# Order of PSUM copies, weight splits and side work in the mixer of a one-core transformer layer

## The chip, the cores and the metric

One core of a Trainium2 chip runs the whole layer as one program. TensorE (PE), VectorE (DVE), ScalarE (ACT), GpSimd (POOL) and SyncE (SP) each work through an instruction queue of their own and meet at semaphores. The metric is device time in microseconds (us), lower is better; a measurement of the kernel is the median of several executions.

## The reference

A "macaron" layer for one sequence of 256 tokens and width 2048: a gated feed-forward block (ffn1), a token mixer and a second feed-forward block (ffn2), each fed through a layer norm that is shifted and scaled by vectors computed from a conditioning vector `c`.

```python
ada = (silu(c) @ w_ada + b_ada)[:, None, :]            # 2048 x 18432
sh1, sc1, g1, sh2, sc2, g2, sh3, sc3, g3 = split(ada, 9)
h = swiglu(modulate(x, sh1, sc1), ffn1_w_in, ffn1_w_out)       # inner width 5632
x = layernorm(ALPHA * x + 0.5 * (1 + g1) * h, ln1_g, ln1_b)
h = token_mixer(modulate(x, sh2, sc2), w_in, ..., w_out)
x = layernorm(ALPHA * x + (1 + g2) * h, ln2_g, ln2_b)
h = swiglu(modulate(x, sh3, sc3), ffn2_w_in, ffn2_w_out)
x = layernorm(ALPHA * x + 0.5 * (1 + g3) * h, ln3_g, ln3_b)

def token_mixer(h, ...):
    z = h @ w_in       # columns: fox q, k, v, f; mLSTM q, k, v, i, f, o
    y_fox = 8 heads of causal softmax attention (width 128) with a decay from cumsum(log_sigmoid(f))
    hm    = 4 heads of chunked mLSTM (width 256; causal conv and silu on q and k), rms-normed
    y     = concat(y_fox, sigmoid(o) * hm)
    return y @ w_out
```

Everything is in float32.

## The kernel before

**Products.** Every product is made from split operands: `split` writes a rounded part `hi` (ACT, L142) and the rest `lo = x - hi` (DVE, L143), and `mm3` adds three products hi·hi, hi·lo, lo·hi (L373 to L375). Weights stream from memory once, one megabyte per `load_w`: SP issues the transfer into one of three `raw` buffers, ACT and DVE split it into `hi` and `lo` tiles of a ring of six. `cols_form_a` uses weights as the stationary operand (256 columns per block of eight rows of 128), `cols_form_b` uses the activations as the stationary operand (blocks of four rows of 128; column groups of two halves [256, 264], so that the small gate columns ride along, or of one half [512]).

**PSUM.** Five banks (`pm`) hold the sums of the big products and three (`pa`, `aux_tile`) everything small. A column group of `cols_form_b` with two halves takes four of the five `pm` banks, so the next group finds one bank free and gets the others as the group before is copied out by `use_fv`, `use_mv` or, for the first group, by the eight sigmoids of L1144, which empty the banks of the mLSTM gate product `mo`.

**The ada vectors.** `w_ada` is contracted on DVE: an accumulation `acc += silu(c)[k] * w_ada[k]` (L157) for each 512 KB row piece, sixteen per part of 1024 columns, then a split and a sum over partitions by PE (`bc`, L170). ffn1's first vectors are made by `first_ada` during the first stage, where ffn1's first 3072 columns (12 groups of 512) are multiplied in four passes over a quarter of the depth each (`first_in`, passes j = 0 to 3; in passes 1 to 3 the add of L749 empties the banks). All others hang on a queue that `pump(rate)` moves on at each weight block; rates are R_F, R_IN and so on, a PAUSE ends a pump early and its debt is carried over. `need(n)` forces the queue on until n parts are done: `need(6)` before j = 9 of ffn2's first half. `pinned()` wraps queue work and adds order edges behind the last noted instructions in `pin`.

**The mixer's side work.** Generators in the list `side` (gates, convolution, mLSTM heads, rms norm, mLSTM outputs, fox heads) are advanced two steps per weight block by `step()`. A generator that yields True waits and does not count. A fox head has three steps: scores `lps` and softmax, transposes `ptp`, value product `yps`. `until(names)` advances in pairs until named steps are done; it is called for buffers and by `before(k)`, ahead of each block of the output projection, for rows k and k + 1 of its input. The projection's rows of the fox heads are split into `yhi` and `ylo`, whose pool takes the place of the mixer's input `xT`.

**Order.** A scheduler orders each engine's queue by estimated readiness and program order. `tc.issue_after(ins)` adds edges: what the block issues on the engine of `ins` comes behind it in that queue, without waiting for its end. `keep_in_program_order` puts an instruction behind everything traced before it on its engine.

Of the kernel before, what the change touches and what calls it, by code (L numbers as in the profile page):

```python
# [34 lines left out]
def layer_kernel(  # L35
# [324 lines left out]

    def load_w(src, nk, w, name):
        raw = wp.tile([P, nk, w], F32, tag="raw", bufs=3, name=f"raw_{name}")
        SP.dma_start(raw, src.rearrange("(k p) n -> p k n", p=P))
        h = nk // 2 if nk * w <= 2048 else nk // 4
        for q in range(nk // h):
            hi = wp.tile([P, h, w], F32R, tag="hi", bufs=6, name=f"hi_{name}{q}")
            lo = wp.tile([P, h, w], F32R, tag="lo", bufs=6, name=f"lo_{name}{q}")
            pin["w"] = split(raw[:, q * h:(q + 1) * h, :], hi, lo).ins
            for kk in range(h):
                yield q * h + kk, hi[:, kk, :], lo[:, kk, :]  # L370
# [6 lines left out]

    def cols_form_a(src, c0, outs, xT, name, npump, halves=(0, 1)):
        xhi, xlo = xT
        for kh in halves:  # L380
            for k8, hi, lo in load_w(src[kh * 1024:(kh + 1) * 1024, c0:c0 + 256], 8, 256, f"{name}_{kh}"):
                k = kh * 8 + k8
                for f in range(2):
                    fs = slice(f * P, (f + 1) * P)
                    mm3(outs[f], hi[:, fs], lo[:, fs], xhi[:, k, :], xlo[:, k, :],
                        k == 8 * halves[0], k == 8 * halves[-1] + 7)
            npump()

# [224 lines left out]

    def cols_1024(raws, xs, split_, load, ps, xT, npump, u0, u1):
        for a in range(2):
            for u, raw in enumerate(raws):
                for q in range(2):
                    k = 2 * u + q
                    for b in range(2):
                        PE.matmul(ps[a, b], xs[a, k], raw(q, b), start=k == 2 * u0, stop=False)  # L620
        for u in range(u0 + len(raws), u1):
            for k, hi, lo in split_.get(u) or load(u):
                for a in range(2):
                    ts_ = slice(a * P, (a + 1) * P)
# [15 lines left out]

    R_F, R_IN, R_OUT, R_MX, R_A, R_B = 1.25, 1.2, 1, 1.42, .9, .6
    NP = 2
# [90 lines left out]
    def first_in(j, i, ws):  # L733
# [9 lines left out]
        for b, ps in enumerate(pss):  # L743
            f0 = 2 * NS * gu + 4 * q + 2 * b
            part = first_part(f0, f0 + 2).rearrange("p f t -> p (f t)")
            if j == 0:
                S.copy(part, ps)
            else:
                V.tensor_tensor(out=part, in0=part, in1=ps, op=ALU.add)  # L749
# [95 lines left out]


    mps = {(a, b): mm_tile(f"mo{a}{b}") for a in range(2) for b in range(2)}
    with tc.issue_after(fence.ins):
        cols_1024(raws, xs, mow, mo_load, mps, xT, at(R_MX), 0, 8)
    npool.release()  # L850
# [15 lines left out]


    side = []
    done = set()

    def advance(n):
        for g in list(side):
            if n == 0:
                break
            got = next(g, 0)
            if got == 0:
                side.remove(g)
            n -= got is not True

# [4 lines left out]

    def step():
        pump(R_MX)
        advance(NP)

# [4 lines left out]

    def cols_form_b(c0, col, ws, use, name):
        ps = {(a, b): mm_tile(f"b_{name}{col}{a}{b}") for b in range(len(ws)) for a in range(2)}
        cb = [sum(ws[:b]) for b in range(len(ws) + 1)]
        for u in range(4):
            for k4, hi, lo in load_w(W[u * 512:(u + 1) * 512, c0 + col:c0 + col + cb[-1]], 4, cb[-1],
                                     f"{name}{col}_{u}"):
                k = u * 4 + k4  # L900
                for a in range(2):
                    ts_ = slice(a * P, (a + 1) * P)
                    for b in range(len(ws)):
                        bs = slice(cb[b], cb[b + 1])
# [24 lines left out]

    def form_a_pair(ca, cb, name):  # L930
        ps = [mm_tile(f"pr_{name}{i}") for i in range(2)]
        cols_form_a(W, ca, [p[:, :T] for p in ps], xT, f"{name}a", step)
        cols_form_a(W, cb, [p[:, T:] for p in ps], xT, f"{name}b", step)
        return ps
# [4 lines left out]
    def use_fv(col, a, ps, w):  # L939
        wv = min(w, 1024 - col)  # L940
        S.copy(yF[:, col // P:(col + wv) // P, a * P:(a + 1) * P], ps[:, :wv].rearrange("p (h n) -> p h n", n=P))
        if wv < w:
            S.copy(gz[:, a, 0:8], ps[:, wv:w])
# [11 lines left out]
    def fox_head(qs, h):  # L955
# [20 lines left out]
        done.add(f"qs{h}")  # L976
        yield
        tps = aux_tile(f"ptp{h}")
        for i in range(3):
# [20 lines left out]
    def use_mv(col, a, ps, w):  # L1000
        wv = min(w, 1024 - col)
        for i in range(0, wv, MV):
            S.copy(yM[(col + i) // MV][:, a, :MV], ps[:, i:i + MV])
# [138 lines left out]
    for a in range(2):  # L1142
        for h in range(NMH):
            S.activation(og[h][:, a, :MV], mps[a, h // 2][:, h % 2 * MV:(h % 2 + 1) * MV], AF.Sigmoid)  # L1144
    cols_form_b(C_FV, 512, [256, 264], use_fv, "fv")
# [24 lines left out]
    for j in (2, 3, 0, 1):  # L1170
        ps = form_a_pair(C_FQ + j * 256, C_FK + j * 256, f"f{j}")
        for i in range(2):
# [4 lines left out]
            side.append(fox_head(qs, h))  # L1177
    cols_form_b(C_FV, 0, [512], use_fv, "fv")
    done.add("fv0")
# [165 lines left out]
```

## Time and profile before

| | |
|---|---|
| three runs | 1955.89, 1961.45, 1962.55 us; median 1961.45 |
| profiled execution | 1965.73 us, its span 1964.0 us |
| granted TensorE clock, mean | 0.993 |
| busy us: PE, DVE, ACT, POOL | 1894.8, 1495.0, 962.6, 41.1 |
| read from memory | 506.71 MB, 259 GB/s over the span |
| mixer, us from the start | input products 843 to 1106, output projection 1110 to 1198 |

The page gives busy time per engine and the waits; a wait is idle time of an engine and the instruction that ended it. A busy PE need not be PE at its full rate: the start-to-start time of its products and the granted clock show that.

### The profile page before, as it was taken

Reading aid. Unit: us, or ns where it says so; the run is one execution under the profiler, and the core shown is the slowest. Engines: PE = TensorE matmul, PEld = TensorE weight load, DVE = VectorE, ACT = ScalarE, POOL = GpSimd, SP = SyncE. Lnnn points to the kernel's source line nnn. Section 1 sums busy time; section 2 is a strip of 40 time slices with the busy share of each in tenths; the row PEclk is TensorE's granted clock in tenths of the full one; section 3 lists DMA queues with packets and bytes.
Section 4 is the critical chain, followed back from the end, with each engine's and each line's share of the span. In section 5 each row is a group of like instructions: output and inputs, shape, how many; then the busy total and the mean of one; then the engine's idle time right before and its main releaser. Section 6 shows DMA issues by size and latency. Waiting matters only on the chain.

```text
span 1964.0 us, 32295 instructions
## 1 busy us (share of the span) xinstructions
PE 1894.8 (96%) x13057; PEld 1726.1 (88%) x13057; DVE 1495.0 (76%) x1878; ACT 962.6 (49%) x1396; POOL 41.1 (2%) x65
## 2 busy tenths in 40 slices
PE   3999999999999999999999998999999999999997
PEld 3999999999988887588999786899999999988885
DVE  7788988777788997677888688767766655555776
ACT  4554454444444554745655544555444444444553
POOL 1211100000000000000000000000000000000000
PEclk9999999999999999999999999999999999999998
DMA  9988878899999785489888784888777765655552
GB/s 351 356 302 293 318 243 290 287 312 315 298 323 322 266 301 173 149 303 299 269 300 278 268 282 157 291 280 278 241 248 250 259 217 190 235 193 193 193 193 86
DMA packets 295677, 510.90 MB, mean 260 GB/s; under 512 B 10818, under 2 KB 158690, under 8 KB 294504
## 3 DMA queue, kind: packets, MB, share of 16 engines
q1 hardware_dynamic: 287752, 480.53, 72.5%
q0 software_dynamic: 7776, 28.32, 4.0%
q8 instruction: 102, 1.67, 0.3%
q14 instruction: 47, 0.39, 0.1%
HBM read 506.71 MB, written 2.10 MB: 259 GB/s over the span
## 4 chain that ended last, share of the span: by engine, by line
PE 82%; DVE 7%; DMA 6%; issue 2%; ACT 2%; SPq 0%; DVEq 0%; POOL 0%; ACTq 0%; POOLq 0%
PE gu_f L373 8%; PE gu_f L375 8%; PE o_f L373 8%; PE gu_f L374 8%; PE o_f L375 8%; PE o_f L374 8%; DMA ar<-in_w_ada_dram 4%; PE s L373 3%; PE s L375 3%; PE s L374 3%; DVE acc L157 2%; PE fs L373 1%; PE fs L374 1%; PE fs L375 1%; PE o_mx L373 1%
## 5 line engine op out<-in xcount | busy, mean ns | idle before, releaser
L157 DVE SCALAR_TENSOR_TENSOR acc<-ar,csil,acc 128x1024 f32<-128x1024 f32 x242 | 307.6, 1272 | 83.2 <-DMA ar<-in_w_ada_dram 82.2
L373 PE MATMUL s<-xhi_f,hi_s 128*128 128x256 f32 x768 | 213.9, 280 | 3.0 <-DVE hT L749 1.3
L375 PE MATMUL s<-xhi_f,lo_s 128*128 128x256 f32 x768 | 213.2, 278 | 0.0
L374 PE MATMUL s<-xlo_f,hi_s 128*128 128x256 f32 x768 | 213.1, 278 | 0.0
L375 PE MATMUL gu_f<-xhi_f,lo_f2i 128*128 128x256 f32 x768 | 212.0, 276 | 0.0
L373 PE MATMUL gu_f<-xhi_f,hi_f2i 128*128 128x256 f32 x768 | 212.0, 276 | 0.0
L374 PE MATMUL gu_f<-xlo_f,hi_f2i 128*128 128x256 f32 x768 | 212.0, 276 | 0.0
L143 DVE TENSOR_TENSOR lo_f2i<-raw_f2i,hi_f2i 128x1024 fp32r<-128x1024 f32 x96 | 117.5, 1224 | 91.6 <-ACT hi_f2i L142 91.6
L373 PE MATMUL gu_f<-xhi_f,hi_f1i 128*128 128x256 f32 x640 | 176.8, 276 | 0.3 <-DVE hT L749 0.3
L375 PE MATMUL gu_f<-xhi_f,lo_f1i 128*128 128x256 f32 x640 | 176.7, 276 | 0.0
L374 PE MATMUL gu_f<-xlo_f,hi_f1i 128*128 128x256 f32 x640 | 176.7, 276 | 0.0
L142 ACT CAST hi_f2i<-raw_f2i 128x1024 fp32r<-128x1024 f32 x96 | 100.8, 1050 | 135.4 <-PE gu_f L374 124.6
L142 ACT CAST hi_s<-raw_s 128x1024 fp32r<-128x1024 f32 x96 | 99.7, 1051 | 113.5 <-PE s L374 60.4
L373 PEld LDWEIGHTS s<-xhi_f,hi_s 128*128 128x128 f32 x768 | 145.3, 190 | 3.7 <-DVE hT L749 1.5
L375 PEld LDWEIGHTS s<-xhi_f,lo_s 128*128 128x128 f32 x768 | 145.1, 189 | 0.3 <-DVE lo_s L143 0.3
L374 PEld LDWEIGHTS s<-xlo_f,hi_s 128*128 128x128 f32 x768 | 145.3, 189 | 0.0
L373 PEld LDWEIGHTS gu_f<-xhi_f,hi_f2i 128*128 128x128 f32 x768 | 144.2, 188 | 0.2
L374 PEld LDWEIGHTS gu_f<-xlo_f,hi_f2i 128*128 128x128 f32 x768 | 144.2, 188 | 0.2
L375 PEld LDWEIGHTS gu_f<-xhi_f,lo_f2i 128*128 128x128 f32 x768 | 144.2, 188 | 0.0
L142 ACT CAST hh<-hT 128x512 fp32r<-128x512 f32 x130 | 80.1, 623 | 130.2 <-PE o_f L374 128.8
L143 DVE TENSOR_TENSOR lo_f2o<-raw_f2o,hi_f2o 128x1024 fp32r<-128x1024 f32 x88 | 107.7, 1224 | 44.9 <-ACT hi_f2o L142 44.8
L373 PE MATMUL o_f<-hi_f2o,hh 128*128 128x512 f32 x344 | 135.2, 393 | 0.0
(453 smaller groups left out, 5400.6 us busy)
## 6 DMA issues: line engine op xcount, KB each, us to landing
ar<-in_w_ada_dram SPq DMA_DIRECT2D x240, 512.0 KB, 5.4
raw_s<-in_ffn_w_in_dram SPq DMA_DIRECT2D x48, 1024.0 KB, 7.5
raw_f2i<-in_ffn_w_in_dram SPq DMA_DIRECT2D x48, 1024.0 KB, 5.1
raw_f1o<-in_ffn_w_out_dram SPq DMA_DIRECT2D x44, 1024.0 KB, 7.5
raw_f2o<-in_ffn_w_out_dram SPq DMA_DIRECT2D x44, 1024.0 KB, 5.1
raw_f1i<-in_ffn_w_in_dram SPq DMA_DIRECT2D x40, 1024.0 KB, 7.6
ar<-in_w_ada_dram POOLq DMA_DIRECT2D x48, 512.0 KB, 6.9
raw_mxo<-in_w_out_dram SPq DMA_DIRECT2D x16, 1024.0 KB, 6.3
```

The costliest lines, as they stand in the source:

```text
L142: S.copy(hi, src)
L143: return V.tensor_tensor(out=lo, in0=src, in1=hi.bitcast(F32), op=ALU.subtract)
L157: V.scalar_tensor_tensor(out=acc, in0=raw, scalar=csil[:, k:k + 1], in1=acc, op0=ALU.mult, op1=ALU.add)
L373: PE.matmul(o, ah, bh, start=start, stop=False)
L374: PE.matmul(o, ah, bl, start=False, stop=False)
L375: PE.matmul(o, al, bh, start=False, stop=stop)
```

## The change

- `load_w` takes `behind`: in `cols_form_b`, the casts of blocks 1 to 3 of a group are ordered behind the last ACT instruction that empties the group before (`emptied`). `use_fv`, `use_mv` return that instruction; `use_mv` takes its gate columns out by two ACT copies, with the two DVE additions of the bias behind them.
- A one-column sigmoid is issued in `cols_1024`, two weight blocks before the end of the `mo` product.
- For fox pairs j = 0 and 1 and the last fox-v group, side work goes one step at half a block and one at its end; the half step leaves out the generator that the last step moved. Fox heads 4 to 7 let one round pass between scores and transposes.
- `first_in`'s add is noted in `pin`, so queue work traced after it is ordered behind it on DVE.
- `R_A`, the rate during ffn2's first half, goes from 0.9 to 1.05.

```diff
-    def load_w(src, nk, w, name):
+    def load_w(src, nk, w, name, behind=None):
...
-            pin["w"] = split(raw[:, q * h:(q + 1) * h, :], hi, lo).ins
+            with ExitStack() as s:
+                if behind:
+                    s.enter_context(tc.issue_after(behind))
+                pin["w"] = split(raw[:, q * h:(q + 1) * h, :], hi, lo).ins
...
-    def cols_form_a(src, c0, outs, xT, name, npump, halves=(0, 1)):
+    def cols_form_a(src, c0, outs, xT, name, npump, halves=(0, 1), mid=None):
...
+                if mid and k8 == 3:
+                    mid()
...
-    def cols_1024(raws, xs, split_, load, ps, xT, npump, u0, u1):
+    def cols_1024(raws, xs, split_, load, ps, xT, npump, u0, u1, ready=None):
...
+            if u == u1 - 2 and ready:
+                ready()
...
-    R_F, R_IN, R_OUT, R_MX, R_A, R_B = 1.25, 1.2, 1, 1.42, .9, .6
+    R_F, R_IN, R_OUT, R_MX, R_A, R_B = 1.25, 1.2, 1, 1.42, 1.05, .6
...
-                V.tensor_tensor(out=part, in0=part, in1=ps, op=ALU.add)
+                pin["h"] = V.tensor_tensor(out=part, in0=part, in1=ps, op=ALU.add).ins
...
+    def sigmoid_table():
+        q = sm.tile([P, 1], F32, tag="rq1", name="rq_table")
+        tc.keep_in_program_order(S.activation(q, c15, AF.Sigmoid))
...
-        cols_1024(raws, xs, mow, mo_load, mps, xT, at(R_MX), 0, 8)
+        cols_1024(raws, xs, mow, mo_load, mps, xT, at(R_MX), 0, 8, sigmoid_table)
...
-    def advance(n):
+    def advance(n, but=()):
+        went = []
         for g in list(side):
             if n == 0:
                 break
+            if g in but:
+                continue
             got = next(g, 0)
             if got == 0:
                 side.remove(g)
-            n -= got is not True
+            if got is not True:
+                went.append(g)
+                n -= 1
+        return went
...
-    def step():
+    def step(n=NP):
         pump(R_MX)
-        advance(NP)
+        moved[:] = advance(n)
+
+    def half_step():
+        advance(NP - 1, moved)
...
-    def cols_form_b(c0, col, ws, use, name):
+    def cols_form_b(c0, col, ws, use, name, by_halves=False):
...
-                                     f"{name}{col}_{u}"):
+                                     f"{name}{col}_{u}", behind=emptied[0] if u else None):
...
-            step()
+                if by_halves and k4 == 1:
+                    half_step()
+            step(1 if by_halves else NP)
...
-                use(col + cb[b], a, ps[a, b], ws[b])
+                emptied[0] = use(col + cb[b], a, ps[a, b], ws[b]).ins
...
+        if h >= 4:
+            yield True
         tps = aux_tile(f"ptp{h}")
...
-            V.tensor_tensor(out=gz[:, a, 12:16], in0=ps[:, wv:wv + 4], in1=gbias[:, 8:12], op=ALU.add)
-            V.tensor_tensor(out=gz[:, a, 8:12], in0=ps[:, wv + 4:w], in1=gbias[:, 12:16], op=ALU.add)
+            S.copy(gz[:, a, 12:16], ps[:, wv:wv + 4])
+            out_ = S.copy(gz[:, a, 8:12], ps[:, wv + 4:w])
+            V.tensor_tensor(out=gz[:, a, 8:12], in0=gz[:, a, 8:12], in1=gbias[:, 12:16], op=ALU.add)
+            V.tensor_tensor(out=gz[:, a, 12:16], in0=gz[:, a, 12:16], in1=gbias[:, 8:12], op=ALU.add)
+        return out_
...
-            S.activation(og[h][:, a, :MV], mps[a, h // 2][:, h % 2 * MV:(h % 2 + 1) * MV], AF.Sigmoid)
+            emptied[0] = S.activation(og[h][:, a, :MV], mps[a, h // 2][:, h % 2 * MV:(h % 2 + 1) * MV],
+                                      AF.Sigmoid).ins
...
-        ps = form_a_pair(C_FQ + j * 256, C_FK + j * 256, f"f{j}")
+        ps = form_a_pair(C_FQ + j * 256, C_FK + j * 256, f"f{j}", j < 2)
...
-    cols_form_b(C_FV, 0, [512], use_fv, "fv")
+    cols_form_b(C_FV, 0, [512], use_fv, "fv", True)
```

More of the change, by code (lines that the diff above doesn't have):

```diff
@@ L869, in layer_kernel @@
     done = set()
-    def advance(n):
+    moved = []
+    def advance(n, but=()):
+        went = []
         for g in list(side):
@@ L891, in wait @@
             yield True
-    def cols_form_b(c0, col, ws, use, name):
+    emptied = [None]
+    def cols_form_b(c0, col, ws, use, name, by_halves=False):
         ps = {(a, b): mm_tile(f"b_{name}{col}{a}{b}") for b in range(len(ws)) for a in range(2)}
@@ L927, in cumsum_col, with form_a_pair @@
         V.tensor_copy(dst, ps[:, :2 * n].rearrange("p (a n) -> p a n", a=2))
-    def form_a_pair(ca, cb, name):
+    def form_a_pair(ca, cb, name, by_halves=False):
+        args = dict(mid=half_step) if by_halves else {}
+        after = (lambda: step(1)) if by_halves else step
         ps = [mm_tile(f"pr_{name}{i}") for i in range(2)]
-        cols_form_a(W, ca, [p[:, :T] for p in ps], xT, f"{name}a", step)
-        cols_form_a(W, cb, [p[:, T:] for p in ps], xT, f"{name}b", step)
+        cols_form_a(W, ca, [p[:, :T] for p in ps], xT, f"{name}a", after, **args)
+        cols_form_a(W, cb, [p[:, T:] for p in ps], xT, f"{name}b", after, **args)
         return ps
@@ L940, in use_fv @@
         wv = min(w, 1024 - col)
-        S.copy(yF[:, col // P:(col + wv) // P, a * P:(a + 1) * P], ps[:, :wv].rearrange("p (h n) -> p h n", n=P))
+        out_ = S.copy(yF[:, col // P:(col + wv) // P, a * P:(a + 1) * P],
+                      ps[:, :wv].rearrange("p (h n) -> p h n", n=P))
         if wv < w:
-            S.copy(gz[:, a, 0:8], ps[:, wv:w])
+            out_ = S.copy(gz[:, a, 0:8], ps[:, wv:w])
             V.tensor_tensor(out=gz[:, a, 0:8], in0=gz[:, a, 0:8], in1=gbias[:, 0:8], op=ALU.add)
+        return out_
     lg = mx.tile([P, 2, 12], F32, name="lg")
@@ L1002, in use_mv @@
         for i in range(0, wv, MV):
-            S.copy(yM[(col + i) // MV][:, a, :MV], ps[:, i:i + MV])
+            out_ = S.copy(yM[(col + i) // MV][:, a, :MV], ps[:, i:i + MV])
         if wv < w:
-            V.tensor_tensor(out=gz[:, a, 12:16], in0=ps[:, wv:wv + 4], in1=gbias[:, 8:12], op=ALU.add)
-            V.tensor_tensor(out=gz[:, a, 8:12], in0=ps[:, wv + 4:w], in1=gbias[:, 12:16], op=ALU.add)
+            S.copy(gz[:, a, 12:16], ps[:, wv:wv + 4])
+            out_ = S.copy(gz[:, a, 8:12], ps[:, wv + 4:w])
+            V.tensor_tensor(out=gz[:, a, 8:12], in0=gz[:, a, 8:12], in1=gbias[:, 12:16], op=ALU.add)
+            V.tensor_tensor(out=gz[:, a, 12:16], in0=gz[:, a, 12:16], in1=gbias[:, 8:12], op=ALU.add)
+        return out_
     acol = mx.tile([P, 2, 4], F32, name="acol")
```

## The prediction

> **What bounds the kernel now.** I read the page's table of engines first, then the waits of PE (engine, line, releaser: total us, times, longest), then the busy time by stretches (length; busy us and instructions of PE, PEld, DVE, ACT, POOL; granted clock; DMA share; GB/s), then timelines around each wait.
>
> ```profile
> PE 1894.8 (96%) x13057; PEld 1726.1 (88%) x13057; DVE 1495.0 (76%) x1878; ACT 962.6 (49%) x1396; POOL 41.1 (2%) x65
> PE bps L108 <- DMA brow<-in_b_ada_dram: 16.2, 1, 16.2
> PE cp L700 <- DVE gate L157: 13.1, 1, 13.1
> PE tp L338 <- DVE n L332: 10.3, 2, 5.1
> PE b_mv L373 <- ACT yF L941: 2.5, 1, 2.5
> PE b_mv L373 <- ACT yM L1003: 1.8, 1, 1.8
> PE ptp L980 <- DVE gate L210: 1.6, 1, 1.6
> PE s L373 <- DVE hT L749: 1.3, 1, 1.3
> PE bc L170 <- ACT ahi L142: 1.3, 1, 1.3
> PE b_fv L373 <- ACT og L1144: 1.3, 1, 1.3
> PE sps L1082 <- DVE dm L1088: 1.2, 1, 1.2
> PE gu_f L373 <- DVE hT L749: 0.3, 1, 0.3
> 1400.00:1500.00 100.00, 100.00 (x883) 99.91 (x882) 68.46 (x84) 44.16 (x53) 0.00 (x0) 1.00 0.72 237
> ```
>
> PE is the bound: it works 1894.8 of 1964.0 us. In an undisturbed stretch it issues 883 products in 100 us, 0.1132 us each, and nothing in this change removes a product. So the most that can be gained is the idle 69 us, and most of that is out of reach: 16.2 and 13.1 us stand at the start, 10.3 us at the two layer-norm boundaries, which the change leaves alone. What it can touch are the eight small waits below these, 11.3 us together, and PE time lost without a wait, which needs the clock column.
>
> **Bank copies and sigmoid table.** Three of the waits stand where a column group of the mixer begins and its banks still hold the group before. The timeline of ACT (start, length, engine, line, operation; in brackets the idle time before it) shows what ACT does there:
>
> ```profile
> 832.48 0.63 ACT L142 CAST hi_fv<-raw_fv 128x520 fp32r<-128x520 f32 x1 [1.92 <-PE mo L375]
> 842.47 0.63 ACT L142 CAST hi_fv<-raw_fv 128x520 fp32r<-128x520 f32 x1 [3.82 <-DMA raw_fv<-in_w_in_dram]
> 843.12 1.28 ACT L1144 ACT_TABLE_LOAD   x1
> 844.41 2.32 ACT L1144 ACTIVATE og<-mo 128x256 f32<-128x256 f32 x8
> 867.92 0.17 ACT L943 COPY gz<-b_fv 128x8 f32<-128x8 f32 x1
> 870.99 0.62 ACT L142 CAST hi_mv<-raw_mv 128x520 fp32r<-128x520 f32 x1 [2.89 <-DMA raw_mv<-in_w_in_dram]
> 871.52 0.64 ACT L941 COPY yF<-b_fv 128x256 f32<-128x256 f32 x2
> 895.30 1.04 ACT L142 CAST hi_mv<-raw_mv 128x1024 fp32r<-128x1024 f32 x1 [2.93 <-DMA raw_mv<-in_w_in_dram]
> ```
>
> Each time a cast of the next group's second weight block sits ahead of the copies in ACT's queue and waits 2.9 to 3.8 us for its DMA; the copies, and PE behind them, wait for a transfer that neither needs. At 843.12 a table load of 1.28 us is added. The change queues the casts of blocks 1 to 3 behind the last copy of the group before. Queued behind that wait are then those casts, their DVE subtractions, and PE's fifth weight row onwards; block 0 holds four rows of 12 products, 48 x 0.1132 = 5.4 us, against about 2.3 us of copies (the eight sigmoids), so PE does not reach them early. The dummy sigmoid puts the 1.28 us load into a queue whose next idle gaps are 1.92 us and more. use_mv's two extra copies per half cost ACT 0.17 us each; the group behind them needs one bank beside the spare one, which is freed before them, and what they cost without that is 0.7 us. I take all three waits as gone: 1.3 + 2.5 + 1.8 = **5.6 us**; at worst 0.3 us each remains (half a pair of copies), 4.7.
>
> [...]
>
> **The order edge in the first stage, and R_A.** The start of ffn1's tail and the end of ffn2's first half:
>
> ```profile
> 308.23 1.29 DVE L157 SCALAR_TENSOR_TENSOR acc<-ar,csil,acc 128x1024 f32<-128x1024 f32 x1 [1.69 <-DMA ar<-in_w_ada_dram]
> 309.44 1.28 DVE L749 TENSOR_TENSOR hT<-hT,s 128x512 f32<-128x512 f32 x2
> 1323.03 1.28 DVE L157 SCALAR_TENSOR_TENSOR acc<-ar,csil,acc 128x1024 f32<-128x1024 f32 x1 [0.30 <-DMA ar<-in_w_ada_dram]
> 1324.35 0.62 ACT L142 CAST ahi<-acc 128x512 fp32r<-128x512 f32 x1 [1.07 <-DVE acc L157]
> 1260.00:1400.00 140.00, 138.64 (x1112) 133.71 (x1112) 106.22 (x126) 73.89 (x117) 0.00 (x0) 1.00 0.84 281
> ```
>
> The add that empties two banks stood behind an accumulation that waited 1.69 us for its own DMA. With the edge the accumulation goes behind the add: 1.3 + 0.3 = **1.6 us** (at worst 0).
>
> At 1323.03 the last accumulation of the sixth ada part is forced just before PE wants its sum. Counting the pump's debt in the code: at 0.9 per block two of the sixteen accumulations are left when need(6) comes, at 1.05 none. So the cast starts about two accumulations earlier and the wait of **1.3 us** goes (at worst 0.9). Two to three accumulations, and their loads of 512 KB on SP's queue between the weight loads, move forward into a stretch where DVE is busy 106 of 140 us and the DMA share is 0.84; both cover them, and without room each would cost its 1.28 us on DVE.
>
> **The fox heads.** Followed step by step through the queue of side work, the change separates what one advance(2) issued together. In the kernel before, the last block of fox-v issues the score products of heads 1 and 2 together:
>
> ```profile
> 1106.40:1110.10 3.70, 3.70 (x18) 2.35 (x16) 1.86 (x5) 3.45 (x8) 0.00 (x0) 1.00 0.94 334
> 1110.10:1113.50 3.40, 3.40 (x8) 2.65 (x9) 3.25 (x10) 2.30 (x9) 0.00 (x0) 0.50 1.00 417
> 1046.30:1054.30 8.00, 6.19 (x40) 4.84 (x39) 6.89 (x11) 5.85 (x13) 0.00 (x0) 1.00 0.71 222
> 1067.22:1072.83 5.61, 5.61 (x49) 5.61 (x49) 4.68 (x9) 2.85 (x7) 0.00 (x0) 1.00 0.91 314
> 1049.84 0.55 PE L980 MATMUL ptp<-ident,s 128*128 128x128 f32 x3 [1.55 <-DVE gate L210]
> ```
>
> Right after these 3.7 us of small f32 products the granted clock is 0.50 for 3.4 us: 8 products where the full rate gives twice as many, so **1.7 us** lost with no wait to show it. In the changed order heads 1 and 2 lie a block apart, and I take the loss as gone; at worst the dip moves to 1046 to 1054, where transposes, a wait and a head's scores still follow one another (0 gained).
>
> [...]
>
> The wait at 1049.84 (three auxiliary banks, held by an ada sum and two transposes, wanted by a fourth tile) stays: at that spot two transposes are still forced by until(), and a score tile takes the place of the fourth. I count 0, with 1.6 as the other end. The wait at sps is untouched.
>
> What it costs: five more places where PE leaves the weight products for small ones. A whole form-a block of 48 takes 5.61 us against 5.43 at 0.1132, so 0.18 each: **0.9 us** (0 to 1.8).
>
> Two covers go. First, out-projection starts on rows 4 and 5, whose parts overwrite the space of xT and so come after the last fox-v product. Second, head 3 now ends one block later, directly ahead of the block that needs it; before, a whole block lay between.
>
> ```profile
> 1106.19 0.40 PE L375 MATMUL b_fv<-hi_fv,xlo_mx 128*128 128x512 f32 x1
> 1107.11 1.14 ACT L142 CAST yhi<-yF 128x512 fp32r<-128x512 f32 x2
> 1107.76 0.69 DVE L143 TENSOR_TENSOR ylo<-yF,yhi 128x512 fp32r<-128x512 f32 x1 [1.59 <-ACT yhi L142]
> 1151.09 0.38 PE L991 MATMUL yps<-pT,yF 128*128 128x128 f32 x2
> 1152.21 0.62 ACT L142 CAST yhi<-yF 128x512 fp32r<-128x512 f32 x1
> 1153.08 0.68 DVE L143 TENSOR_TENSOR ylo<-yF,yhi 128x512 fp32r<-128x512 f32 x1
> ```
>
> The first: last product 1106.59, first cast half done about 1107.7, low part 1108.45. The score products covered it; with three transposes alone in between I take **0.9 us** (0 if ready weights of another block go first, 1.9 with no cover). The second: from 1151.47 to 1152.83 for the high part, 1153.77 for the low: **1.4 us** (0 if products of the next group fill the spare bank, 2.3).
>
> **Sum.** 5.6 + 1.6 + 1.3 + 1.7 = 10.2 gained, 0.9 + 0.9 + 1.4 = 3.2 given back: 7.0 us. The profiled execution took 1965.7 us (span 1964.0 and 1.7 around it), so 1958.7; it lay 0.22% above the median of the three runs, 1961.45, and on the median's scale this is 1954.4 us.
>
> **The rivals.** *Given back* (the same): the clock dip moves to 1046 to 1054 (1.7), both covers cost their upper ends (1.0 and 0.9 more), the splits 1.8. Then 7.0 - 1.7 - 1.9 - 0.9 = 2.5 us remain, 1963.2 in the profile, 1958.9. For it: the forced stretch stays, with 1.8 us of PE idle in 8. Against: a scheduler that orders by readiness fills holes it foresees.
>
> *DVE starved by the new edge* (slower).
>
> ```profile
> 180.00:240.00 60.00, 60.00 (x532) 60.00 (x531) 56.66 (x61) 23.60 (x24) 9.38 (x13) 1.00 0.91 319
> 179.53 1.29 DVE L749 TENSOR_TENSOR gate<-gate,s 128x512 f32<-128x512 f32 x2 [1.12 <-PE s L375]
> ACT hi_s L142 <- PE s L374: 60.4, 45, 3.9
> ```
>
> In the first stage DVE is busy 56.66 of 60 us, so it has 0.30 us to spare per group of 48 products (5.43 us). Now accumulations may no longer fill the time until PE finishes a group. If each of the 24 groups of the second and third passes waits 1.12 us like the row at 179.53, 0.82 x 24 = 19.7 us are lost, 12.7 net: 1978.4, or 1974 on the median's scale. It decides once DVE's lost time passes 0.30 us per group on average. Against it: the casts wait 60.4 us for PE to free weight buffers, so weights are ready groups ahead, and only an average over groups counts. The accumulations' buffers also come free later, so their loads start later: on POOL's queue in the second and third pass, and on SP's in the fourth, where a load that waits for its buffer holds the weight loads queued behind it.
>
> *The dip stays* (same): 1.7 us less, 5.3 gained, 1960.4, or 1956.1. [...]
>
> *The edges do not bite* (same): copies still come late because something else holds ACT; 7.0 - 5.6 = 1.4 us, 1964.3, or 1960.0. Against: only those casts stood ahead of them.
>
> **How the numbers follow.** About 0.3% (5.9 us) is what a measurement of this kernel can tell from no change. Forecast 0.62, of which 0.06 falls short of 5.9 us; given back 0.17; starved 0.10; dip stays 0.07; edges 0.04. So faster 0.56, same 0.06 + 0.17 + 0.07 + 0.04 = 0.34, slower 0.10. Best end: 10.2 + 1.6 (ptp) with no cost, 11.8 us, 1949.7; a little below for the short waits about these. Worst of the same-sided cases: 4.7 + 0.9 gained, 6.0 lost, 1961.9. The range 1947 to 1963 leaves out the slower rival.
>
> **What would show it.** Right: no wait of b_fv on og, nor of b_mv on yF or yM; table load before 840; no clock below 1 between 800 and 1195; hT and bc gone from PE's waits; a new small wait of o_mx on yhi or ylo. Wrong: PE waiting on lo_s or hi_s before 300; a dip near 1050; b waits still there.

## The result, and the profile after

| | median, us | lowest to highest | profiled execution, us | span, us |
|---|---|---|---|---|
| before | 1961.45 | 1955.89 to 1962.55 (5 runs) | 1965.73 | 1964.0 |
| changed | 1970.81 | 1964.01 to 1974.42 (5 runs) | 1968.63 | 1966.8 |

The ratio of the two is 1.0044, 95% interval 1.0028 to 1.0061: the change makes the kernel some 9 us slower. The prediction said 1954.4 us, 7 us faster, with 1947 to 1963 as its range. It was wrong in sign. The two profiled executions lie only 2.9 us apart (1965.73 is above the median of its kernel, 1968.63 below), so what the profiles show below accounts for a net 2.8 us of the 9.

The waits of PE in the changed kernel (engine, tile, line, releaser: total us, times, longest us), without the waits at the start and at the layer norms, which are as before:

```profile
PE yps L1025 <- ACT yF L972: 5.1, 1, 5.1
...
PE lps L996 <- DVE gate L210: 1.8, 1, 1.8
PE bc L170 <- DVE alo L143: 1.5, 2, 1.2
PE o_mx L376 <- DVE res L443: 1.5, 1, 1.5
PE pr_m L378 <- DVE lo_m1b L143: 1.4, 1, 1.4
PE b_mv L377 <- DVE lo_mv L143: 1.2, 1, 1.2
...
```

The three waits that the change aims at (b_fv on og, b_mv on yF and on yM) are not in the list, and the waits on hT from DVE have gone too. In their place stand others, of those shown all but one on DVE, and one long one: a head's value product `yps` waits 5.1 us for the copies `yF` on ACT. A second view shows where the time went: the start and end of the mixer's stages, read from the timeline of PE.

| us from the span's start | before | changed | ahead by |
|---|---|---|---|
| first product of the mixer (mo) | 787.8 | 785.0 | 2.8 |
| mLSTM values begin (b_mv) | 868.2 | 862.8 | 5.4 |
| query and key pairs begin (pr_m) | 920.9 | 912.1 | 8.8 |
| last fox-v product ends | 1106.6 | 1100.5 | 6.1 |
| output projection begins (o_mx) | 1110.0 | 1108.7 | 1.3 |
| output projection ends | 1207.0 | 1209.7 | -2.7 |
| span | 1964.0 | 1966.8 | -2.8 |

(The projection of the kernel before ends at 1207.0, not at 1198 as the table ahead of the prediction has it.) Up to the pairs the changed kernel is 8.8 us ahead. It loses 2.7 us among the pairs and fox-v, 4.8 us between the last fox-v product and the output projection, and 4.0 us inside the projection. All that is lost is lost behind the beginning of the pairs.

The 4.8 us, in four queues. Each line is start, length, engine, line and operation, with the idle time before it and its releaser in brackets; the timelines of PE, ACT, DVE and SP of the changed kernel around 1100:

```profile
1100.12 0.40 PE L378 MATMUL b_fv<-hi_fv,xlo_mx 128*128 128x512 f32 x1
1105.57 1.22 PE L1025 MATMUL yps<-pT,yF 128*128 128x256 f32 x2 [5.05 <-ACT yF L972]
1104.41 0.62 ACT L142 CAST ahi<-acc 128x512 fp32r<-128x512 f32 x1 [5.53 <-DVE acc L157]
1104.94 1.07 ACT L972 COPY yF<-b_fv 128x512 f32<-128x512 f32 x2
1093.06 1.27 DVE L157 SCALAR_TENSOR_TENSOR acc<-ar,csil,acc 128x1024 f32<-128x1024 f32 x1
1103.09 1.28 DVE L157 SCALAR_TENSOR_TENSOR acc<-ar,csil,acc 128x1024 f32<-128x1024 f32 x1 [5.30 <-DMA ar<-in_w_ada_dram]
1093.16 0.38 SPq L363 DMA_DIRECT2D raw_mxo<-in_w_out_dram  x1
1094.36 0.33 SPq L200 DMA_DIRECT2D ar<-in_w_ada_dram  x1
```

Read it from the bottom. The accumulation of 1093.06 frees one of the two ada buffers at 1094.33; SP issues the next load into it at once, 1.2 us behind a weight load of 1 MB; 8.4 us after the end of that issue DVE can do the last accumulation of that ada part, having stood idle 5.30 us for it. ACT has the cast of that sum, `ahi`, at the head of its queue and stands 5.53 us. Behind the cast stand the copies of the fox-v banks, which were complete at 1100.52. PE's next instruction, `yps`, reads what they write. In the profile before, the same cast ran at 1100.67 after 0.44 us, and sixteen score products, 3.6 us, covered the copies on PE.

The granted clock adds to it (length; busy us and instructions of PE, PEld, DVE, ACT, POOL; granted clock; DMA share; GB/s; windows of the changed kernel):

```profile
1037.40:1043.90 6.50, 4.11 (x27) 3.00 (x26) 5.22 (x7) 3.91 (x7) 0.00 (x0) 1.00 0.95 327
1043.90:1047.30 3.40, 3.40 (x16) 3.18 (x16) 3.25 (x10) 2.36 (x7) 0.00 (x0) 0.51 0.77 239
1105.40:1112.20 6.80, 6.63 (x16) 5.05 (x17) 3.23 (x5) 2.96 (x6) 0.00 (x0) 0.50 0.62 242
```

PE runs at half rate for 3.4 us after a stretch with 2.4 us of waits, and for 6.8 us behind the 5 us wait: 1.7 and 3.4 us of work lost, by the clocks of 0.51 and 0.50. Between 800 and 1200 the kernel before has one such dip, 3.4 us at 1110.1 with a clock of 0.50, and loses 1.7 us by it.

The last 4.0 us, inside the projection, are not the clock: 3.5 us of the second dip fall into it, but the dip of before lay in its projection too, with 3.4 us. They are one wait (1.46 us before the o_mx product at 1166.73) and 2.6 us more of work. The first line is before's projection, the second the changed one's:

```profile
1110.00:1207.00 97.00, 96.96 (x422) 78.30 (x421) 76.02 (x96) 39.74 (x63) 0.55 (x1) 0.98 0.75 261
1108.70:1209.70 101.00, 99.53 (x430) 79.30 (x429) 76.45 (x99) 41.20 (x66) 0.55 (x1) 0.98 0.72 242
```

The added work is score products that come later: 21 of them instead of 9 run inside the projection. DVE ahead of the wait:

```profile
1163.00 1.28 DVE L157 SCALAR_TENSOR_TENSOR acc<-ar,csil,acc 128x1024 f32<-128x1024 f32 x1 [2.66 <-DMA ar<-in_w_ada_dram]
1164.20 0.69 DVE L441 TENSOR_TENSOR o_mx<-o_mx,gate 128x512 f32<-128x512 f32 x1
1164.80 1.27 DVE L157 SCALAR_TENSOR_TENSOR acc<-ar,csil,acc 128x1024 f32<-128x1024 f32 x1
1166.00 0.68 DVE L443 SCALAR_TENSOR_TENSOR res<-res,o_mx 128x512 f32<-128x512 f32 x1
```

Again an accumulation that waits for its load (2.66 us), and a second one, stand ahead of the two adds that empty PE's bank.

### The profile page after: what moved, and what is told of

It reads as the page before. It is cut to its first block, busy times and chain, and to the rows that moved or that the text cites. A ratio compares the mean times of both kernels' runs of the same rounds, so it can differ in the third digit from the quotient of the medians.

```text
span 1966.8 us, 32294 instructions
## 1 busy us (share of the span) xinstructions
PE 1894.9 (96%) x13057; PEld 1726.4 (88%) x13057; DVE 1494.3 (76%) x1878; ACT 963.7 (49%) x1401; POOL 41.1 (2%) x65
## 4 chain that ended last, share of the span: by engine, by line
PE 82%; DMA 8%; DVE 5%; ACT 2%; issue 2%; SPq 0%; DVEq 0%; POOL 0%; ACTq 0%; POOLq 0%
PE gu_f L377 8%; PE gu_f L376 8%; PE o_f L376 8%; PE gu_f L378 8%; PE o_f L378 8%; PE o_f L377 8%; DMA ar<-in_w_ada_dram 6%; PE s L376 4%; PE s L378 4%; PE s L377 4%; DVE acc L157 2%; PE fs L377 1%; PE fs L378 1%; PE fs L376 1%; PE pr_f L376 1%
## 5 line engine op out<-in xcount | busy, mean ns | idle before, releaser
L143 DVE TENSOR_TENSOR lo_s<-raw_s,hi_s 128x1024 fp32r<-128x1024 f32 x96 | 115.8, 1220 | 25.5 <-ACT hi_s L142 25.4
```

Of the source, the lines that this page charges most:

```text
L143: return V.tensor_tensor(out=lo, in0=src, in1=hi.bitcast(F32), op=ALU.subtract)
```

## The experiments

Medians are compared through each kernel's ratio to the kernel before, measured beside it on the same chip; 0.001 is 2.0 us.

**First set: which part of the change costs.** The theory: the fox heads' half steps take the covers away, and an ada cast in ACT's queue does the rest. Rivals: the order edges starve DVE, or the copies in front bring nothing.

*a1: the changed kernel without half steps and extra round.*

```diff
-        if h >= 4:
-            yield True
...
-        ps = form_a_pair(C_FQ + j * 256, C_FK + j * 256, f"f{j}", j < 2)
+        ps = form_a_pair(C_FQ + j * 256, C_FK + j * 256, f"f{j}")
...
-    cols_form_b(C_FV, 0, [512], use_fv, "fv", True)
+    cols_form_b(C_FV, 0, [512], use_fv, "fv")
```

> The changed kernel without the half steps and without the extra round of heads 4 to 7; copies, table, order edge and R_A stay. Theory H (the half steps cost it: their order puts a value product that needs the fox-v copies right behind the last fox-v product, where two heads' scores stood before): the 5.1 us wait before the output projection is gone, and the kernel is 6 to 9 us faster than the one before (5.6 copies and table, 1.6 edge, 1.3 R_A). Rival D (PE that is earlier only meets the ada transfers earlier, the gain is handed back as a wait on them): within 3 us of the kernel before, with a wait of several us near 1100 whatever the order of heads.

*a2: the kernel before with the half steps and the extra round alone* (the lines that a1 removes, with the code of the half steps, put into before).

> The kernel before with the half steps and the extra round alone. Theory H: slower than the kernel before by 5 to 10 us, with the wait of the value product on the fox-v copies, about 5 us, and clock dips behind it. Rival D: PE is not earlier than before, so the transfers are not late; the wait is under 2 us and the time within 3 us of the kernel before.

*a3: the changed kernel with the ada casts ordered behind the copies of the last fox-v group.*

```diff
     cols_form_b(C_FV, 0, [512], use_fv, "fv", True)
+    pin["e"] = emptied[0]
```

> The changed kernel with one more order edge: ada casts traced after the last fox-v group queue behind its two bank copies on ACT. Theory S (the copies stand behind an ada cast that waits for its accumulation and that for a DMA): the wait of 5.1 us falls under 1.5 us, the dip of 6.8 us after it goes or halves, and the time is 5 to 9 us below the changed kernel. If the lost cover alone made the wait (no cast in the way), the time stays within 2 us of the changed kernel.

*a4: the kernel before with the copies in front and the early table alone* (`load_w`'s `behind`, `emptied`, `sigmoid_table` and the copies in `use_mv`).

> The kernel before with the copies ahead of later casts and the early table alone. As forecast: 5 to 6 us faster than the kernel before, the three waits of b_fv and b_mv gone. Rival D: the three waits go but return as a wait on transfers later in the mixer, time within 2 us of the kernel before.

| | median, us | ratio to before | 95% interval |
|---|---|---|---|
| changed | 1970.81 | 1.0044 | 1.0028 to 1.0061 |
| a1, no half steps | 1957.33 | 0.9981 | 0.9973 to 0.9990 |
| a2, half steps alone | 1975.65 | 1.0067 | 1.0051 to 1.0083 |
| a3, late ada cast | 1965.51 | 1.0021 | 1.0008 to 1.0033 |
| a4, copies and table alone | 1958.96 | 0.9989 | 0.9980 to 0.9998 |

The half steps with the extra round cost 0.0067 on the old kernel and 0.0063 on the new one, 12 to 13 us; without them the change is a gain of 3.7 us, less than the 6 to 9 that I had expected. The profile of a1, 10.1 us shorter in span, shows where: its last fox-v product ends level with the changed kernel's (1100.3 against 1100.5), and the 5.05 us wait, the 3.4 us that the clock takes behind it and the 1.46 us wait in the projection, none of which a1 has, make 9.9 of the 10.1. In a2 the same long wait stands in PE's list, beside two of the three old ones:

```profile
PE yps L1023 <- ACT yF L970: 4.4, 1, 4.4
PE b_mv L376 <- ACT yF L970: 2.5, 1, 2.5
...
PE b_fv L376 <- ACT og L1178: 1.0, 1, 1.0
```

Putting the cast behind the copies (a3) takes the wait of yps away and wins 0.0023, 4.5 us (by the intervals, some 4 more or less), but its time comes back in part where the sum is wanted and where the cast's neighbours are late:

```profile
PE bc L170 <- ACT ahi L142: 3.4, 1, 3.4
PE o_mx L378 <- DVE ylo L143: 2.9, 1, 2.9
1104.48 0.62 ACT L142 CAST ahi<-acc 128x512 fp32r<-128x512 f32 x1 [2.68 <-DVE acc L157]
1105.27 0.62 ACT L142 CAST yhi<-yF 128x512 fp32r<-128x512 f32 x1
```

The late cast now stands one place further back, ahead of the second half of `yhi`, and PE waits 2.9 us for the low part made from it. So a third of the cost goes with the long wait, and the lateness itself stays. The copies and the table win 2.2 us (0.4 to 3.9), not 5.6. PE now waits instead on low parts of weights: in a1, 2.8 us in all on `lo_m1b`:

```profile
945.39 1.28 DVE L157 SCALAR_TENSOR_TENSOR acc<-ar,csil,acc 128x1024 f32<-128x1024 f32 x1 [1.83 <-DMA ar<-in_w_ada_dram]
946.59 2.46 DVE L1093 SCALAR_TENSOR_TENSOR o<-u,hcol,o 128x256 f32<-128x256 f32 x6
948.97 2.35 DVE L143 TENSOR_TENSOR lo_m1b<-raw_m1b,hi_m1b 128x1024 fp32r<-128x1024 f32 x2
```

PE reaches these products earlier, and DVE, held by an accumulation and by the convolution, does not.

**Second set: which of the half steps.** All four start from a1.

*c1: half steps in the two fox pairs only* (`j < 2` is back); *c2: in the last fox-v group only* (`True` is back); *c3: the extra round of heads 4 to 7 only* (`if h >= 4: yield True` is back).

> The changed kernel with half steps in the two fox pairs alone (none in the last fox-v group, no extra round). Its order behind the last fox-v product is two heads' scores, as in the kernel before. Theory V (what costs is that a value product, and not scores, follows the last fox-v product): no wait there, time within 2 us of the kernel without any half steps (1957). Theory N (the many switches between weight products and small products cost it, wherever they are): 5 us or more above 1957.

> The changed kernel with half steps in the last fox-v group alone. Its order behind that group is two value products and an ada sum. Theory V: a wait of 3 to 5 us there on the fox-v copies, a clock dip behind it, 6 to 12 us above the kernel without half steps. Theory N: 2 to 4 us above it, spread, no long wait.

> The changed kernel without half steps, but with the extra round of heads 4 to 7 between scores and transposes. Its order behind the last fox-v group is one transpose and one value product, then scores only a block later. Theory V: the same wait as with half steps, 3 to 5 us, and a dip; 6 to 12 us above the kernel without either. Theory N: within 1 us of that kernel, since nothing is split up.

*e1: another pace for the ada queue*, so that accumulations move out of the mixer's second half.

```diff
-    R_F, R_IN, R_OUT, R_MX, R_A, R_B = 1.25, 1.2, 1, 1.42, 1.05, .6
+    R_F, R_IN, R_OUT, R_MX, R_A, R_B = 1.25, 1.2, 1.1, 1.32, 1.05, .6
```

> The changed kernel without half steps and extra round, with the ada rate 1.1 instead of 1 in ffn1's second product and 1.32 instead of 1.42 in the mixer. Theory D (in the mixer PE, once earlier, waits for weights that stand behind accumulations waiting for their transfers): the wait of pr_m on lo_m1b, 1.7 to 2.8 us, shrinks, and the time falls 1 to 3 us under the kernel with the old rates (1957). Rival: no gain, since ffn1's second product has no DMA time to spare either.

| | median, us | ratio to before | 95% interval | above a1 |
|---|---|---|---|---|
| c1, pairs | 1959.48 | 0.9988 | 0.9978 to 0.9997 | 1.4 us |
| c2, fox-v | 1962.31 | 1.0004 | 0.9994 to 1.0013 | 4.5 us |
| c3, extra round | 1963.29 | 1.0010 | 0.9994 to 1.0027 | 5.7 us |
| e1, pace | 1963.26 | 1.0002 | 0.9990 to 1.0014 | 4.1 us |

The three add up to 11.6 of the 12.4 us, each known to some 2 to 4 us, so there is no single culprit among them and no sign of an effect that needs all three. Theory V holds for c1 and nearly gives c3's time, c2 lies next to theory N: neither holds alone. I had expected the 5 us wait in c2. It is not there, although its transposes and value products do follow the last fox-v product (which ends at 1104.29) as foreseen. The cast `ahi` waits 3.04 us for its sum there too, but it is through 6 us before the copies:

```profile
1098.32 0.62 ACT L142 CAST ahi<-acc 128x512 fp32r<-128x512 f32 x1 [3.04 <-DVE acc L157]
1104.80 0.57 ACT L972 COPY yF<-b_fv 128x512 f32<-128x512 f32 x1
1105.42 1.23 PE L1023 MATMUL yps<-pT,yF 128*128 128x256 f32 x4
```

So it is not the order of PE's products alone that makes the long wait; a late cast at that place has to come to it. Where c2's 4.5 us go instead was not followed up. In c3 yps waits for another copy, and a slow stretch follows, in which PE's products start some 0.43 us apart until 1104.45, against 0.23 us behind it:

```profile
1101.29 1.22 PE L1025 MATMUL yps<-pT,yF 128*128 128x256 f32 x2 [2.39 <-ACT pT L1020]
```

On ACT an ada cast again stood 2.37 us ahead of that copy. e1 is a miss: the pace moves accumulations elsewhere, and waits come up there (sps on dm 4.0 us, o_f on lo_f1o 2.9 us).

**Third set: the ada accumulations.** In the long waits looked at so far an accumulation or its cast stood in a queue. d1 to d3 leave half of those beside the mixer out.

```diff
-                raw = ap.tile([P, 2, 512], F32, tag="araw", bufs=2, name=f"ar{v}_{j}_{k}")
-                SP.dma_start(raw, src[k * P:(k + 1) * P])
-                ada_acc(acc, raw, k)
+                if v == 3 or j > 1 or k % 2 == 0:
+                    raw = ap.tile([P, 2, 512], F32, tag="araw", bufs=2, name=f"ar{v}_{j}_{k}")
+                    SP.dma_start(raw, src[k * P:(k + 1) * P])
+                    ada_acc(acc, raw, k)
```

(In `ada_gate` the same with `v != 5 or k % 2 == 0`. What these kernels put out lacks half of the terms of these sums.)

*d1: this in the kernel before. d2: this in a4. d3: this in the changed kernel. f1: a1 with a3's line* (nothing left out).

> The kernel before, without every second accumulation (and its 512 KB load) of the ada parts that run beside the mixer (gate 5 and the first two column blocks of pair 6: 32 of 64 left out, the output is not the reference's). It is the base for the next two. Both theories: PE is the bound and the accumulations lie on DVE beside it, so little changes: 1955 to 1961 us, the three waits of b_fv on og, b_mv on yF and b_mv on yM still there, because weight loads and not ada loads hold them.

> The kernel before with the copies in front and the early table, and the same 32 accumulations left out. Theory: of the forecast 5.6 us only some 2 came because weight parts on DVE now stand behind accumulations that wait for ada loads (pr_m on lo_m1b, b_mv on lo_mv); with half of these loads gone those waits shrink below 1 us together and it is 4 to 6 us below the kernel with the same left out. Rival: the waits that went were worth only about 2 us anyway, since PE catches up elsewhere; then it is 1.5 to 3 us below.

> The changed kernel with the same 32 accumulations left out. Theory: the 5 us wait of yps on yF comes from a cast of an ada sum that waits for the sum's last load and stands ahead of the bank copies; with half the loads gone that load is early, the wait falls below 2 us, and the kernel is 3 to 6 us above the first of these three instead of 9.4 us. Rival: the half steps cost by themselves (switches, covers, clock dips); then it stays 8 to 10 us above, and the wait is there with another releaser or its time turns up elsewhere.

> The changed kernel without half steps and extra round, and with the ada casts after the last fox-v group ordered behind its copies. Theory: without half steps two heads' scores cover the time in which the ada cast stands ahead of the copies, so the order is worth nothing here: 1955.5 to 1959.5 us, ratio to before 0.997 to 0.999. Rival: putting the casts late is good by itself (it was worth 5 us with the half steps), then 1952 to 1954.5 us.

| | median, us | ratio to before | 95% interval |
|---|---|---|---|
| d1, before, half the accumulations | 1954.52 | 0.9959 | 0.9945 to 0.9973 |
| d2, a4, half | 1952.78 | 0.9950 | 0.9930 to 0.9969 |
| d3, changed, half | 1953.78 | 0.9955 | 0.9939 to 0.9971 |
| f1, a1 with late ada cast | 1958.51 | 0.9980 | 0.9968 to 0.9993 |

This is the main answer. With half of the accumulations gone the three kernels cannot be told apart: the changed one is 0.7 us below before instead of 9.4 above, and the half steps lose most of their price. d3 lies 1.0 us over d2 (the intervals allow some 5 either way), but d3 also has the order edge and the new R_A, which d2 has not and which are worth 1.6 us between a1 and a4; so the half steps may still cost some 2.6 us here, by this estimate, in place of 12 to 13. What is left of them in d3's list is 2.2 us of o_mx on `res`. The long wait is gone: no ada cast stands near the copies, they run as the last fox-v products end, and `yps` follows at once.

```profile
1090.70 1.28 ACT L974 COPY yF<-b_fv 128x512 f32<-128x512 f32 x2 [0.98 <-PE b_fv L380]
1090.95 0.40 PE L380 MATMUL b_fv<-hi_fv,xlo_mx 128*128 128x512 f32 x1
1091.34 0.70 PE L1027 MATMUL yps<-pT,yF 128*128 128x256 f32 x2
```

PE loses nothing any more in the stretch of the fox pairs either. Before, changed, a1, d1 and d3, each the window of 960 to 1060:

```profile
960.00:1060.00 100.00, 96.99 (x778) 92.42 (x778) 88.56 (x158) 63.26 (x124) 0.00 (x0) 1.00 0.84 280
960.00:1060.00 100.00, 97.03 (x766) 92.74 (x767) 85.29 (x155) 60.07 (x120) 0.00 (x0) 0.98 0.82 271
960.00:1060.00 100.00, 96.19 (x773) 92.02 (x773) 86.38 (x154) 60.51 (x119) 0.00 (x0) 1.00 0.82 273
960.00:1060.00 100.00, 100.00 (x802) 95.65 (x802) 78.98 (x147) 61.37 (x121) 0.00 (x0) 1.00 0.67 221
960.00:1060.00 100.00, 100.00 (x810) 96.08 (x809) 78.93 (x141) 59.45 (x114) 0.00 (x0) 1.00 0.70 229
```

Before and a1 lose their 3 to 4 us there as well, so this stretch shows what the accumulations cost every one of these kernels, not the price of the half steps. I had expected 3 to 6 us over d1 to remain in d3; nothing of the kind does. I had also expected d1 to keep the three old waits. Two of them are gone there without the change's order edges; of the three only the wait on `og` is left in its list, and ACT shows why the wait on `yF` is not there:

```profile
PE b_fv L375 <- ACT og L1146: 1.1, 1, 1.1
865.10 0.63 ACT L142 CAST hi_mv<-raw_mv 128x520 fp32r<-128x520 f32 x1 [0.81 <-PE b_fv L377]
865.63 0.64 ACT L943 COPY yF<-b_fv 128x256 f32<-128x256 f32 x2
```

A cast still stands directly ahead of the copies, but its weights are there: in before it had waited 2.89 us for them, here no cast of this stretch waits for a transfer. That is why the copies' gain did not grow in d2 (1.7 us over d1, as the rival said): d1 had it already. f1 equals a1, but that does not show that scores would cover a late cast: in a1's profile `ahi` runs at 1094.08 after 0.49 us, 5 us before the copies, so there was nothing to move.

**Fourth set: the load or the vector time.** g1 keeps the 32 accumulations and drops their loads (each reads again what was loaded for the one before). g2 keeps all loads and lets these accumulations take an eighth of their columns. Both edits are shown for `ada_pair`; `ada_gate` has the same with its own condition.

```diff
# g1
-                raw = ap.tile([P, 2, 512], F32, tag="araw", bufs=2, name=f"ar{v}_{j}_{k}")
-                SP.dma_start(raw, src[k * P:(k + 1) * P])
+                if v == 3 or j > 1 or k % 2 == 0:
+                    raw = ap.tile([P, 2, 512], F32, tag="araw", bufs=2, name=f"ar{v}_{j}_{k}")
+                    SP.dma_start(raw, src[k * P:(k + 1) * P])
                 ada_acc(acc, raw, k)
# g2
-                ada_acc(acc, raw, k)
+                if v == 3 or j > 1 or k % 2 == 0:
+                    ada_acc(acc, raw, k)
+                else:
+                    ada_acc(acc[:, :, 0:64], raw[:, :, 0:64], k)
```

> The changed kernel in which every second accumulation of gate 5 and of the first two column blocks of pair 6 reads again the rows loaded for the one before it: 32 loads of 512 KB are gone, the 32 accumulations on DVE stay (the output is not the reference's). Theory 'loads': the casts of ada sums and the weights wait for transfers, so this recovers nearly what leaving out both did (1953.8 us): 1953 to 1958 us, no wait of yps on yF above 1 us. Rival 'DVE time': each accumulation keeps DVE 1.28 us, and weight parts, gates and scores queue behind it; then 1963 to 1971 us and the clock dips near 1044 and 1105 stay. In between: both.

> The changed kernel in which the same 32 accumulations take only an eighth of their columns, while all loads stay (the output is not the reference's): about 32 x 1.1 us of DVE time gone beside the mixer. Theory 'loads': 1966 to 1971 us, the wait of yps on yF stays at 3 us or more. Rival 'DVE time': 1953 to 1960 us.

g1 took 1958.53 us (ratio 0.9985, 0.9976 to 0.9994), 11.6 us below the changed kernel; g2 1955.19 us (0.9962, 0.9949 to 0.9974), 16.1 us below; leaving out both was 17.5 us below. So neither theory holds alone: taking away either one gives most of it. DVE's waits for ada loads between 780 and 1200, in before, changed, g1 and g2, show how far:

```profile
DVE acc L157 <- DMA ar<-in_w_ada_dram: 24.0, 24, 2.3
DVE acc L157 <- DMA ar<-in_w_ada_dram: 38.3, 27, 5.3
DVE acc L157 <- DMA ar<-in_w_ada_dram: 12.4, 11, 2.5
DVE acc L157 <- DMA ar<-in_w_ada_dram: 27.8, 26, 2.7
```

With two buffers a load is issued when an accumulation ends, and an accumulation runs when its load has landed; each stands in line with the engine's other work. (In the changed kernel the load issued at 1094.36 follows the accumulation that ended at 1094.33, and the accumulation of 1103.09 had DVE idle for 5.30 us ahead of it, until that load was there.) In g2 every load is still made, at the same DMA share (0.82 in the window of 960 to 1060 in both), and yet PE is busy 100.00 of 100 us there and the wait of yps is gone. In g1 DVE is as busy as before the change in that window (89.23 us against 88.56), and PE is busy 100.00 too. So neither DVE's total nor the transfers' total was the limit by itself. What fits both runs is lateness: an accumulation that isn't ready at the head of a queue in which work for PE stands behind it. This is argued, not shown, for g2: its waits for loads still add up to 27.8 us, more than before's 24.0, and only the longest has gone from 5.3 to 2.7.

Three things stay open. Why the sum is late in the changed kernel (its cast at 1104.41) and not in a1 (1094.08) is traced no further than to the load issued at 1094.36. Leaving accumulations out makes the kernel before 8.0 us faster as well (d1), and how that divides between load and vector time was not tried on it. And the scheduler orders by estimates, so a kernel with less work also has other orders: in g2 the cast `ahi` runs at 1086.61, ahead of the copies at 1091.24. Order and load were not separated beyond a3, f1 and the profile of c2.

## Why the prediction was wrong, point by point

**Copies and table: mechanism right, size too large.** All three waits are gone; the copies run right behind the last product. In the profiled executions the stretch from the mixer's first product to the pairs shrinks from 133.1 to 127.1 us, 6.0 against the 5.6 of the sum. The medians give 2.2 us (a4). The step that failed is to take the sum of the three waits, 5.6, as a gain of the whole kernel, twice over: the waits of one execution were taken for those of all (a2 has the old order and shows 2.5 and 1.0, the third is not there), and PE's next release, low parts of weights on DVE, was not asked for (1.7 us on `lo_m1b` in a4). How much each of the two takes from the gain stays open.

**Order edge: right.** The mixer's first product comes 2.8 us earlier in the changed kernel and 2.7 in a1, against 0.6 in a4, which has no edge; 1.6 was forecast. Over all profiles but e1's, whose pace differs ahead of the mixer, it comes at 784.0 to 785.6 with the edge and at 786.0 to 787.9 without. No wait of PE on `lo_s` came up, so DVE had the room.

**R_A: nothing of the 1.3.** The sum's cast starts earlier, but its low part `alo` now waits behind other splits on DVE, and `bc` still waits 1.5 us. a1 is 1.6 us below a4 by the medians, where edge and R_A together were to give 2.9; that fits the edge alone.

**The clock dip: moved and grown.** The step "in the changed order heads 1 and 2 lie a block apart, and I take the loss as gone" failed in its premise. In a1 the same two heads' scores follow one another right after fox-v, and the clock stays whole (windows of a1, the scores and the 3.4 us behind them):

```profile
1100.10:1103.70 3.60, 3.60 (x18) 2.27 (x16) 1.87 (x5) 3.35 (x8) 0.00 (x0) 1.00 1.00 390
1103.70:1107.10 3.40, 3.40 (x16) 2.82 (x16) 3.25 (x10) 2.75 (x10) 0.00 (x0) 1.00 0.86 352
```

So the burst is not enough to make a dip. The worst case named there, a dip at 1046 to 1054, came at 1043.9, and one of 6.8 us came behind the 5 us wait: 5.1 us are lost between 800 and 1200 where the kernel before loses 1.7, so 3.4 us went where 1.7 were to be won. In the 3.4 us ahead of a dip PE was idle for 1.84 us (changed, at 1043.9), for all of them (changed, at 1105.4) and for none (before, at 1110.1). What sets a dip off is not shown by these runs.

**The first cover: the step that failed worst.** It stood in the sum with 0.9 us and 1.9 as its worst case, and measured 5.05 us (4.4 in a2), with 3.4 us of clock behind it. By itself this would not have turned the sign (7.0 - 4.2 = 2.8 us); with the dips' -3.4 in place of +1.7 it does (2.8 - 5.1 = -2.3). All the half steps and the extra round together stood in the sum with 1.5 us net (3.2 given back, 1.7 gained) and cost 12 to 13. Its working began the copies at the last product's end, as in the profile before, and counted cast and low part from there. It never asked what stands ahead of the copies on ACT, although the part on the copies had just shown a cast at the head of that queue holding copies for 2.9 to 3.8 us. In the changed kernel ACT stood idle for 5.53 us ahead of `ahi`, and the copies behind it, whose banks were complete at 1100.52, started at 1104.94. Where no late cast stands there, the lost cover costs next to nothing (d3: `yps` starts at 1091.34, 0.39 us behind the start of the last fox-v product).

**The second cover: size right, place wrong.** 1.4 us were forecast, as a wait of o_mx on `yhi` or `ylo`; 1.5 us came, from the adds that empty a bank behind two accumulations. c3, where a head's last step also comes later, has it too (1.8), and d3 with half of the accumulations still has 2.2.

**Five more switches at 0.9 us** can't be read alone: c1, with half steps in two pairs, is 1.4 us above a1, and the intervals overlap.

**The rivals.** *Given back* had the place of the first new dip nearly right and the covers as what costs, and stopped at 1.9 us for what took 5. *DVE starved* had the right sign and nearly the right time, 1974, by a mechanism that did not occur: it put the lack in the first stage. What it described, accumulations and their loads coming late in a queue, took place in the mixer, where I had not looked for it.

The best version that leaves nothing out is a1: 1957.33 us, ratio 0.9981 to before, copies, table, edge and rate without the half steps (f1 equals it).

## What to carry to other kernels

Before a cover is taken away, read the whole queue of the engine whose result it hid: the price is not only the length of that result's chain but also the wait of any instruction ahead of it (here ACT's 5.53 us ahead of one cast). Background work that stands in the queues of the critical path (here 512 KB loads with an accumulation each) had PE wait 5.05 us where one sum came late and nothing covered it; halving it in the kernel before was worth 8.0 us, the best change of order 3.7. Ask, too, whether an order alone makes a wait: c2 has the order that was feared, and not the wait. A sum of waits from one profiled execution is not yet a gain (5.6 us here, 2.2 by the medians): ask for each wait what PE waits for next, and whether a second execution shows the wait at all.

## What the runs showed of the hardware

Between 800 and 1200 us the granted clock was at half once in the kernel before (0.50 for 3.4 us at 1110.1) and twice in the changed one (0.51 for 3.4 us at 1043.9, 0.50 for 6.8 us at 1105.4). In the 3.4 us ahead of these three PE was idle for 0, 1.84 and 3.4 us. Such idle time did not always bring a dip: in before, 1.8 us of it fell into the 8 us from 1046.3, and the clock was 1.00 there and in the 20 us from 1060. The same burst of small products without a wait had a dip behind it in before (0.50 from 1110.1) and none in a1 (1.00 from 1103.7). An ada load of 512 KB was used 8.4 us after the end of its issue when it was issued 1.2 us behind a 1 MB load (changed, issue at 1094.36); the profile page's median for these loads is 5.5 us to landing.
